# A split QKV matmul on one core: the direct columns of each pair of row blocks moved ahead of its first products

## The chip, the cores and the metric

The kernel runs on one core of a Trainium2 chip. The metric is the device time in microseconds (us) from start to end of one execution; for several executions it is the median. A profiled execution of the same program gives the trace that is read here.

## What is computed

`x` is 16 x 512 x 768 and `w_qkv` is 768 x 2304, both float32. Cut to what matters:

```python
qkv = np.matmul(x, w_qkv)                 # (16, 512, 2304)
q, k, v = qkv[..., :768], qkv[..., 768:1536], qkv[..., 1536:]
return np.stack([q, k, v], axis=0)        # (3, 16, 512, 768), float32
```

So it is one product of an 8192 x 768 matrix with a 768 x 2304 matrix, written out as three blocks of columns.

## The kernel before

**Tiles.** The 8192 rows are taken 256 at a time, as 32 "pairs" of two 128-row blocks, numbered p = 0 to 31. The 2304 columns are cut into two groups of 1024 (called q = 0 and q = 1, each two blocks of 512) and 256 columns between them, the "direct columns". For each pair and each group, `quad(p, q)`, the 2 x 2 block product (two row blocks, two halves of the inner dimension, two column blocks) is formed from seven block products instead of eight: sums of blocks of x (tile `s`, made on GpSimd) are multiplied by sums of blocks of w (`t1` to `t4`, made once). Products 1 and 2 are in bf16 and take x from the tile `xb`; products 3 to 7 are in float32r and take the sums `s`. Each product is 3 matmuls of 512 columns. The direct columns are computed plainly by `rem(p)`: 12 bf16 matmuls of 256 columns (L260), one eviction on ScalarE (L270, `orem`) and one store of 256 KB on the queue of SP (L271).

**Stages.** A prologue loads and casts w, computes pairs 0 to 2 plainly in bf16 (`block`, L396) and stores them (`store_quad`). Pairs 3 to 30 then run in a loop over p, each by `two(a, b, early)`, where a is the group q = 0 and b the group q = 1 of the same pair. Pair 31 is done by `last`. In `last`, the two halves of the direct columns follow float32r products.

**Who does what in a pair.** `do(u, n)` issues product n on TensorE (L210) and its evictions. ACT is ScalarE and DVE is VectorE.

- Product 1 opens the PSUM bank `u.x`, which ACT copies out (L224). Products 6, 7 and 4 go on accumulating into `u.x`, each after ACT has copied the state before (L231, L237, L241).
- Product 2 has its own bank `u.z`, which DVE adds to the output (L228).
- Product 5 opens the bank `u.y`. DVE adds it to the output after product 7 (L238). Product 3 then accumulates into `u.y`, so it must wait for that L238, and DVE adds it again (L244).
- `store_quad` writes a group out as two stores on SP: L251 (768 KB) and L252 (256 KB) for a, L255 (256 KB) and L256 (768 KB) for b.
- `early()` prepares x for later pairs. DVE transposes x of pair p + 1 (L130), GpSimd (POOL) rounds it to bf16 (L173, `xb`) and makes the sums (L181 to L185), and the x of pair p + 2 is loaded in four pieces of 192 KB (L126), two issued by SP and two by ACT.

**Order.** Each engine runs its instructions in the order in which the program writes them (the schedule is manual). The loads and stores of SP and ACT signal their landing on eight completion semaphores, which the layer under the kernel hands out in rotation; a transfer waits on its issuing engine until the last transfer with the same semaphore has landed. PSUM has eight banks, taken in rotation by `ps_pool`; a pair takes seven. The output tiles `o` have five buffers, `orem` two, `xin` three, `xf` two, `xb` four.

The line that makes product 3 wait, and the one that the change moves, stand in `do` and `two`:

Of the kernel before, what the change touches and what calls it, by code (L numbers as in the profile page):

```python
# [10 lines left out]
def kernel(  # L11
# [131 lines left out]
    def copy_halves(dst, src, two):  # L143

        nc.vector.tensor_copy(out=dst[0], in_=src[0])
        if two:
            nc.scalar.activation(dst[1], src[1], ident)
        else:
            nc.vector.tensor_copy(out=dst[1], in_=src[1])
# [3 lines left out]
    def cast_row(p, r, two=True):  # L153
        if r == 0:
            xc[p] = s_pool.tile([P, 2, K], bf16, name="xc", tag="s")
        halves = (slice(0, K // 2), slice(K // 2, K))
        copy_halves([xc[p][:, r, n] for n in halves], [xin[p][:, r, n] for n in halves], two)
# [41 lines left out]
    def product(u, n, ps, start):  # L199
        t1, t2, t3, t4 = ts[u.q]  # L200
        if n <= 2:
            h = (n - 1) * KH
            lhs = [xb[u.p][:, h + j, :P] for j in range(KH)]
            rhs = [b1[u.q][:, h + j, :] for j in range(KH)]
        else:
            k, t = {3: (4, b22[u.q][:]), 4: (0, t4), 5: (1, t1), 6: (2, t2), 7: (3, t3)}[n]
            lhs = [sr[u.p][:, k, j, :] for j in range(KH)]
            rhs = [t[:, j, :] for j in range(KH)]
        for j in range(KH):
            nc.tensor.matmul(  # L210
                ps[:], lhs[j], rhs[j],
                start=(start and j == 0), stop=(j == KH - 1), skip_group_check=True,
            )

    def bank():
        return ps_pool.tile([P, CB], fp32, name="ps")

    def do(u, n):
        c11, c12 = u.o[:, 0, :CB], u.o[:, 0, CB:]
        c21, c22 = u.o[:, 1, :CB], u.o[:, 1, CB:]  # L220
        if n == 1:
            u.x = bank()
            product(u, 1, u.x, True)
            nc.scalar.activation(c11, u.x[:], ident)  # L224
        elif n == 2:
            u.z = bank()
            product(u, 2, u.z, True)
            nc.vector.tensor_tensor(c11, c11, u.z[:], op=add)  # L228
        elif n == 6:
            product(u, 6, u.x, False)  # L230
            nc.scalar.activation(c12, u.x[:], ident)  # L231
        elif n == 5:
            u.y = bank()
            product(u, 5, u.y, True)
        elif n == 7:
            product(u, 7, u.x, False)
            nc.scalar.activation(c22, u.x[:], ident)  # L237
            nc.vector.tensor_tensor(c22, c22, u.y[:], op=add)  # L238
        elif n == 4:
            product(u, 4, u.x, False)  # L240
            nc.scalar.activation(c21, u.x[:], ident)  # L241
        elif n == 3:
            product(u, 3, u.y, False)
            nc.vector.tensor_tensor(c12, c12, u.y[:], op=add)  # L244

    def rows_of(s, p, lo, hi):
        return out_flat[s, p * 2 * P:(p + 1) * 2 * P, lo:hi].rearrange("(r m) n -> m r n", m=P)

    def store_quad(u):
        if u.q == 0:  # L250
            nc.sync.dma_start(rows_of(0, u.p, 0, H), u.o[:, :, :H])  # L251
            nc.sync.dma_start(rows_of(1, u.p, 0, 2 * CB - H), u.o[:, :, H:])  # L252
        else:
            part = 2 * H - Q_OFF[1]
            nc.sync.dma_start(rows_of(1, u.p, H - part, H), u.o[:, :, :part])  # L255
            nc.sync.dma_start(rows_of(2, u.p, 0, H), u.o[:, :, part:])  # L256

    def rem_row(p, r, ps):
        for j in range(KT):
            nc.tensor.matmul(  # L260
                ps, xb[p][:, j, r * P:(r + 1) * P], w_rem[j // KH][:, j % KH, :],
                start=(j == 0), stop=(j == KT - 1), skip_group_check=True,
            )

    def rem(p):
        ps = ps_pool.tile([P, 2, REM], fp32, name="ps")
        for r in range(2):
            rem_row(p, r, ps[:, r, :])
        o = or_pool.tile([P, 2, REM], fp32, name="orem")
        nc.scalar.activation(o[:], ps[:], ident)  # L270
        nc.sync.dma_start(rows_of(1, p, R_OFF - H, R_OFF - H + REM), o[:])  # L271

    def two(a, b, early):

        do(a, 1)
        do(b, 1)
        early()
        rem(a.p)
        do(a, 2)
        do(b, 2)  # L280
        do(a, 6)
        do(b, 6)
        do(a, 5)
        do(a, 7)
        do(b, 5)
        do(b, 7)
        do(a, 4)
        do(a, 3)
        store_quad(a)
        do(b, 4)  # L290
        do(b, 3)
        store_quad(b)
# [183 lines left out]
    for p in range(NS, NP):  # L476
        def early():
            if p + 1 < NP:
                transpose(p + 1)
                round_x(p + 1)  # L480
                sums_x(p + 1)
            if p + 2 < NP:
                load_x(p + 2, nc.scalar)

        if p < NP - 1:
            two(quad(p, 0), quad(p, 1), early)
        else:
            last(quad(p, 0), quad(p, 1))
# [30 lines left out]
```

## Time and profile before

| what | value |
|---|---|
| time, median of 3 runs | 362.73 us (362.62 to 362.82) |
| the profiled execution's own time | 362.66 us |
| its span, first to last instruction | 360.9 us |
| TensorE clock granted | 0.997 of full speed |
| TensorE busy | 354.3 us, 98% of the span |
| DVE, ACT, POOL busy | 224.7, 182.5, 173.5 us |
| moved by DMA | 108.08 MB, 299 GB/s over the span |

The span runs from the first to the last instruction. The time of a run is a little longer, here by 1.8 us. In the profile a line such as "L210 PE MATMUL" names the line of the kernel, the engine (PE is TensorE, PEld its weight loads) and the operation; the last letter of "SPq" or "ACTq" marks an instruction that issues a transfer. Timeline rows give the start and the length in us, and in brackets the idle time of the engine before it with what ended it. Matmul durations overlap each other, since matmuls are pipelined; the distance between starts is what a matmul costs.

### The profile page before, as it was taken

To read this page: it belongs to the slowest core of one execution; us is meant where nothing else is said; L and a number is where in the kernel's file an instruction comes from. 1 tells how busy PE (TensorE), PEld (TensorE's weight loads), DVE (VectorE), ACT (ScalarE), POOL (GpSimd) and SP (SyncE) were. 2 spreads that over 40 slices of the span, in tenths; PEclk is the share of its full clock that TensorE was granted. 3 is DMA by queue.
4 is the path that set the end of the run, shared out by engine and by line. 5 is a ranking of instruction groups with operands and counts; after the bars stand their busy time and mean duration, and the time that the engine had idled before them with its cause. 6 is when DMAs were issued, how large, how long until landed. Compare 5 with 4: busy or idle time off the path is not lost.

```text
span 360.9 us, 5252 instructions
## 1 busy us (share of the span) xinstructions
PE 354.3 (98%) x1797; PEld 250.2 (69%) x1797; DVE 224.7 (62%) x239; ACT 182.5 (51%) x304; POOL 173.5 (48%) x180
## 2 busy tenths in 40 slices
PE   7999999999999999999999999999999999999995
PEld 3544577777777777777777777777777777777763
DVE  3599736765566675566675565676556676556642
ACT  4557554545454545454545444445545454545452
POOL 0001861646664445664445665444665444666410
PEclk9999999999999999999999999999999999999998
DMA  7999969988898999999899999988989899989766
GB/s 299 404 385 369 308 224 360 316 300 293 276 330 303 291 273 296 276 319 311 283 282 287 284 303 312 293 269 297 293 285 323 295 300 271 297 263 339 274 259 235
DMA packets 80634, 108.08 MB, mean 299 GB/s; under 512 B 4833, under 2 KB 60385, under 8 KB 80609
## 3 DMA queue, kind: packets, MB, share of 16 engines
q1 hardware_dynamic: 65200, 96.35, 80.9%
q10 hardware_dynamic: 15408, 11.41, 9.6%
q8 instruction: 14, 0.23, 0.3%
q14 instruction: 12, 0.09, 0.1%
HBM read 32.24 MB, written 75.50 MB: 299 GB/s over the span
## 4 chain that ended last, share of the span: by engine, by line
PE 96%; DMA 2%; ACT 1%; ACTq 0%; SPq 0%; issue 0%; DVE 0%
PE ps L210 75%; PE ps L260 11%; PE ps L396 9%; DMA st<-in_w_qkv_dram 2%; PE ps L165 0%; ACT o L241 0%; ACTq L301 0%; SPq L141 0%; ACT orem L315 0%; DVE b L417 0%; ACTq L317 0%; ACTq L315 0%
## 5 line engine op out<-in xcount | busy, mean ns | idle before, releaser
L210 PE MATMUL ps<-t,s 128*128 128x512 f32 x696 | 173.8, 398 | 0.0
L210 PEld LDWEIGHTS ps<-t,s 128*128 128x128 f32 x696 | 130.7, 188 | 29.8
L173 POOL CAST xb<-xf 128x1536 bf16<-128x1536 f32 x29 | 43.7, 1509 | 168.2 <-DVE xf L130 166.1
L238 DVE TENSOR_TENSOR o<-o,ps 128x512 f32<-128x512 f32 x58 | 39.9, 687 | 90.9 <-ACT o L237 90.9
L130 DVE STREAM_TRANSPOSE xf<-xin 128x1536 f32<-128x1536 f32 x29 | 85.6, 2952 | 4.5 <-DMA xin<-in_x_dram 2.5
L210 PE MATMUL ps<-b,xb 128*128 128x512 bf16 x348 | 84.9, 380 | 0.0
L237 ACT ACTIVATE o<-ps 128x512 f32<-128x512 f32 x58 | 34.7, 598 | 44.3 <-PE ps L210 44.3
L210 PEld LDWEIGHTS <-xb 128*128 128x128 bf16 x348 | 31.7, 98 | 35.6 <-issue 7.3
L231 ACT ACTIVATE o<-ps 128x512 f32<-128x512 f32 x58 | 34.7, 598 | 42.3 <-PE ps L210 39.5
L244 DVE TENSOR_TENSOR o<-o,ps 128x512 f32<-128x512 f32 x58 | 39.9, 688 | 21.4 <-PE ps L210 20.2
L210 PE MATMUL ps<-b,s 128*128 128x512 f32 x174 | 48.7, 389 | 0.0
L260 PE MATMUL ps<-w_rem,xb 128*128 128x256 bf16 x384 | 47.3, 273 | 0.0
L241 ACT ACTIVATE o<-ps 128x512 f32<-128x512 f32 x58 | 34.7, 598 | 24.1 <-PE ps L210 21.3
L224 ACT ACTIVATE o<-ps 128x512 f32<-128x512 f32 x58 | 34.6, 597 | 23.8 <-DVE o L244 20.7
L260 PEld LDWEIGHTS <-xb 128*128 128x128 bf16 x384 | 37.4, 98 | 11.2 <-issue 0.5
L228 DVE TENSOR_TENSOR o<-o,ps 128x512 f32<-128x512 f32 x58 | 36.5, 671 | 4.7 <-PE ps L210 3.4
L210 PEld LDWEIGHTS ps<-b,s 128*128 128x128 f32 x174 | 32.7, 188 | 6.8
L182 POOL TENSOR_TENSOR s<-s,xf 128x384 fp32r<-128x384 f32 x29 | 30.0, 1033 | 2.3
L181 POOL TENSOR_TENSOR s<-xf 128x384 fp32r<-128x384 f32 x29 | 30.8, 1061 | 0.0
L185 POOL TENSOR_TENSOR s<-xf,s 128x384 fp32r<-128x384 f32 x29 | 29.4, 1014 | 0.0
L183 POOL TENSOR_TENSOR s<-xf 128x384 fp32r<-128x384 f32 x29 | 29.4, 1012 | 0.0
L270 ACT ACTIVATE orem<-ps 128x512 f32<-128x512 f32 x31 | 18.5, 597 | 21.2 <-PE ps L260 21.2
(36 smaller groups left out, 128.7 us busy)
## 6 DMA issues: line engine op xcount, KB each, us to landing
out_dram<-o SPq DMA_DIRECT2D x62, 768.0 KB, 5.0
out_dram<-o SPq DMA_DIRECT2D x65, 256.0 KB, 4.2
xin<-in_x_dram SPq DMA_DIRECT2D x62, 192.0 KB, 6.9
xin<-in_x_dram ACTq DMA_DIRECT2D x54, 192.0 KB, 4.4
out_dram<-orem SPq DMA_DIRECT2D x31, 256.0 KB, 5.8
st<-in_w_qkv_dram SPq DMA_DIRECT2D x6, 768.0 KB, 13.0
xin<-in_x_dram SPq DMA_DIRECT2D x3, 768.0 KB, 5.6
st<-in_w_qkv_dram SPq DMA_DIRECT2D x6, 256.0 KB, 6.0
```

Of the source, the lines that this page charges most:

```text
L130: nc.vector.transpose(t[:].rearrange("p j (g b) -> p g j b", b=G), xin.pop(p)[:].rearrange("p g (a j) -> p g j a", a=G),)
L173: nc.gpsimd.tensor_copy(out=xb[p][:], in_=xf[p][:])
L210: nc.tensor.matmul(ps[:], lhs[j], rhs[j], start=(start and j == 0), stop=(j == KH - 1), skip_group_check=True,)
L224: nc.scalar.activation(c11, u.x[:], ident)
L228: nc.vector.tensor_tensor(c11, c11, u.z[:], op=add)
L231: nc.scalar.activation(c12, u.x[:], ident)
L237: nc.scalar.activation(c22, u.x[:], ident)
L238: nc.vector.tensor_tensor(c22, c22, u.y[:], op=add)
L241: nc.scalar.activation(c21, u.x[:], ident)
L244: nc.vector.tensor_tensor(c12, c12, u.y[:], op=add)
L260: nc.tensor.matmul(ps, xb[p][:, j, r * P:(r + 1) * P], w_rem[j // KH][:, j % KH, :], start=(j == 0), stop=(j == KT - 1), skip_group_check= ...
L396: nc.tensor.matmul(ps[n][:], xb[p][:, j, r * P:(r + 1) * P], w[:, j, :], start=(j == 0), stop=(j == KT - 1), skip_group_check=True,)
```

## The change

In `two`, the call `rem(a.p)` moves from after `early()` to the very beginning:

```diff
     def two(a, b, early):
 
+        rem(a.p)
         do(a, 1)
         do(b, 1)
         early()
-        rem(a.p)
         do(a, 2)
         do(b, 2)
         do(a, 6)
```

On TensorE a pair's 12 matmuls of 256 columns now come before its first products, and its four bf16 products of 512 columns stand together, ahead of the float32r ones. On ACT the eviction L270 comes before the two L224, and these before the two load issues. On SP the store L271 comes before the two loads L126 instead of after them. DVE and POOL keep their order. The rotation of PSUM banks and of completion semaphores follows the new order, so some transfers wait for another transfer than before. The second SP load of pair p now waits for the landing of L251 of pair p - 1, which L271 waited for before. Pairs 0 to 2 and pair 31 are not touched.

## The prediction

> **What bounds the kernel now.** I began with the chain of work that ended last, on the profile's page:
>
> ```profile
> PE 96%; DMA 2%; ACT 1%; ACTq 0%; SPq 0%; issue 0%; DVE 0%
> PE ps L210 75%; PE ps L260 11%; PE ps L396 9%; DMA st<-in_w_qkv_dram 2%; PE ps L165 0%; ACT o L241 0%; ACTq L301 0%; SPq L141 0%; ACT orem L315 0%; DVE b L417 0%; ACTq L317 0%; ACTq L315 0%
> ```
>
> It is TensorE from end to end: L210 (products) and L260 (direct columns). In order of time, the same chain shows the loop's period:
>
> ```profile
> 185.94 1.31 PE ps L260 x12
> 187.25 9.43 PE ps L210 x42
> 196.68 1.31 PE ps L260 x12
> 198.00 9.43 PE ps L210 x42
> ```
>
> 1.31 + 9.43 = 10.74 us per pair with nothing in between, so in the loop TensorE never waits. Nothing can be won by taking waits away, and the change costs exactly the stalls it makes. I then looked for where a stall would come first. Per-pair windows show DVE busy 6.9 of 10.74 us, ACT 5.4, POOL 5.9, but the DMA engines 93 to 97%. The thin place is the fourth pair of rows (p = 4; its first matmul starts at 55.60, that of p = 3 at 44.84, of p = 5 at 66.34), in DVE's timeline:
>
> ```profile
> 55.79 0.69 DVE L244 TENSOR_TENSOR o<-o,ps 128x512 f32<-128x512 f32 x1 [0.67 <-PE ps L210]
> 58.43 3.02 DVE L130 STREAM_TRANSPOSE xf<-xin 128x1536 f32<-128x1536 f32 x1 [1.95 <-DMA out_dram<-orem]
> 61.39 1.23 DVE L228 TENSOR_TENSOR o<-o,ps 128x512 f32<-128x512 f32 x2
> 63.08 0.69 DVE L238 TENSOR_TENSOR o<-o,ps 128x512 f32<-128x512 f32 x1 [0.47 <-ACT o L237]
> ```
>
> The transpose of x for p = 5 waited 1.95 us for a transfer. The view names orem, but the program has it wait for the x loads, and the landing record of the second SP load is 58.21. DVE's order puts both L228 and L238 behind it. L238 ends at 63.77; the u.y bank that it reads is what `do(a, 3)` accumulates into next, and that product starts here (TensorE's timeline):
>
> ```profile
> 64.29 0.84 PE L210 MATMUL ps<-b,s 128*128 128x512 f32 x3
> ```
>
> So this transpose may be late by 0.47 (idle before L238) + 0.47 (64.29 - 63.77, less about 0.05 for the signal, an estimate from the 0.04 to 0.09 between a matmul's end and ACT's start) = **0.94 us** and no more. In steady pairs the transpose starts 0.79 us after the pair and DVE idles 2.57 before L238 (0.47 here), so the margin is 3.0.
>
> Why the load was late is in SP's timeline:
>
> ```profile
> 49.48 0.37 SPq L256 DMA_DIRECT2D out_dram<-o  x1
> 49.91 0.46 SPq L255 DMA_DIRECT2D out_dram<-o  x1
> 50.46 0.97 SPq L256 DMA_DIRECT2D out_dram<-o  x1
> 51.52 0.85 SPq L271 DMA_DIRECT2D out_dram<-orem  x1
> 52.47 2.38 SPq L126 DMA_DIRECT2D xin<-in_x_dram  x2
> 54.94 0.48 SPq L271 DMA_DIRECT2D out_dram<-orem  x1
> 55.52 0.45 SPq L251 DMA_DIRECT2D out_dram<-o  x1
> ```
>
> The first L256 (a prologue store) was ready long before; it shares a completion semaphore with the first ACT load of p = 5 (issued 46.41, landed 49.42) and waits for that landing. Everything below is queued behind it.
>
> **What the Trainium skill says.** "DMA: Bandwidth & Descriptors", section "Anatomy of one DMA — SWDGE (gpsimd) path": a semaphore wait is served on the issuing sequencer, before dispatch. The trace agrees: SP holds the whole list until 49.42. The same page, "Queues, rings and completion order": an SDMA engine takes a ring's descriptors in order, though completions need not be. Here the landings do follow SP's order (52.82, 53.53, 55.39, 56.42, 57.60, 58.21, 58.82), so a transfer put ahead delays those after it. "TensorE: Matmul & The Clock Gate", section "Back-to-back issue gap": N/2.4 + 2.5 ns, which is 216 ns for 512 columns and 109 for 256. The trace has 216 and 109 for bf16, and 227 to 232 for float32r. The same section's sustained 131 ns for 512 columns isn't seen here.
>
> **The change part by part.** Nothing is removed or added. In 28 pairs (p = 3 to 30; `last` is untouched), 12 matmuls of rem, its eviction (L270) and its store (L271) move ahead of `do(a, 1)`, `do(b, 1)` and `early()`. DVE and POOL keep their order.
>
> *TensorE.* Twelve times 109 ns move from after six products to before them: 0. The one seam that changes is float32r to bf16, now met by a 256-column product. Before, a 230 ns step and then 227 (216 + 11). In `last`, rem already follows float32r products: 230, then 120 (109 + 11). Equal extra, so 0; at most 28 x 14 ns = 0.4 us either way.
>
> *ACT.* L270 moves ahead of both L224, and both L224 and the two ACT load issues come 1.3 us later. From the steady pair that starts at 195.22, measured from its start: rem's last matmul starts at 1.21, lasts 0.27, so L270 is at 1.52 to 2.12; L224 at 2.22 to 2.81 and 2.86 to 3.46. `do(a, 6)` overwrites u.x at 3.72 and `do(b, 6)` at 4.60: margins 0.9 and 1.1. L228 starts at 3.65 as now: hidden by the transpose. Next on ACT after the issues (2.9 to about 4.2) is L231 at 4.79: free. Should an issue hold ACT past 5.4, `do(a, 7)` at 6.0 would wait.
>
> *PSUM.* Eight banks in rotation, seven taken per pair. Now rem takes the bank of y of b two pairs back, x of a that of rem, z of a that of x of b; the others are unchanged. The latest of these is read out (L241 of b) 0.1 us after the pair's start and needed by z at 2.6: 0.
>
> *SP in steady pairs.* The orem store (issue 1.2 us) goes ahead of the two SP loads, and the second load inherits the wait that orem's store had, for the 768 KB L251 of the pair before (landed 3.0 us after the pair's start). I put all x landings near 10.9, where the orem store now lands, against the transpose at 11.5 and its margin of 3. No trace shows this order; its bounds are 0 below (TensorE has no wait to win back) and the second rival above; I take 0.
>
> *SP and DVE in pairs 3 and 4*: this is the cost.
> 1. ACT load of p = 5. Before, L224 of b started at 46.39 and the issue followed at 46.41. After: rem 44.84 to 46.15, x of a and b to 47.45, L224 of b at 47.23 (last matmul) + 0.38 + 0.09 = 47.69, issue at 47.72, that is 1.31 later. Landing takes 3.0 as before (nothing competes): 50.73.
> 2. The first L256 therefore goes at 50.79, and all below it 1.31 later.
> 3. rem's store of p = 3 (256 KB) now stands before the two loads. The two orem stores of this burst landed 1.03 and 0.61 us after their forerunners; I take 0.8.
> 4. Second load lands at 58.21 + 1.31 + 0.8 = 60.3 (60.1 to 60.6); the transpose starts 0.1 to 0.2 later, at 60.5, which is 2.07 after 58.43.
> 5. Stall at `do(a, 3)`: 2.07 - 0.94 = **1.1 us** (0.8 to 1.5). The upper bound, with the slowest 256 KB store seen near here (1.29), is 1.7.
>
> What is late next: L238 of b has 0.6 to spare, POOL's cast for p = 5 ends near 65.1, before that pair starts at 67.5. Its sums end near 69.6 against 71.2. The loads for p = 6 wait for ACT loads issued 1.3 later; I find their transpose near 69, against a limit of about 71.3 in the shifted pair. So one stall, never given back, as TensorE has no idle time.
>
> **Sum.** The profiled execution took 362.66 us (span 360.9, the rest around it), 0.07 under the median of the runs, 362.73. 362.66 + 1.1 = 363.8 (363.5 to 364.4).
>
> **Rivals.** A measurement of this kernel can tell about 0.2%, 0.7 us.
>
> *Absorbed (not slower).* The load lands in time: if L256's extra wait vanished, because the ACT load lands by 49.5 after all, only orem's 0.8 would remain, below 0.94. It decides at a transpose start of 59.4. For it: the margin exists, and latencies of the same load vary from 3.0 to 7.0. Against it: an idle queue gave 3.0 before, and later issue can hardly land earlier. 362.7.
>
> *Every pair pays.* The second SP load's new wait, or an ACT issue held by a full ring, makes each pair late. At p = 4 an ACT issue took 1.31 us. Point of decision: transpose over 3.0 us late, or ACT held past 5.4. With 0.3 us over it in 27 pairs: +8, 371. Against it: the inherited landing is at 3.0, and the margins above.
>
> *Faster.* The seam vanishes or banks come free earlier. The whole seam is 0.4 us: 362.3. Against it: `last` shows it unchanged.
>
> *The change does not do what it says:* excluded, since the built program shows the moved instructions on TensorE, ACT and SP.
>
> **How the numbers follow.** One stall 0.75, absorbed 0.13, every pair 0.08, faster 0.04. Of one stall about 0.03 lies under 0.7 us; so slower 0.72 + 0.08 = 0.80, same 0.13 + 0.03 + 0.01 = 0.17, faster 0.03. The likeliest: 363.8. The range takes in absorbed and the stall's upper bound with 0.2 to spare, 362.6 to 364.6, and leaves out the last two cases, 0.12.
>
> **What the profile after would show.** Right: the first L256 at 50.8, the transpose of p = 5 near 60.5, L238 after it with no idle, a gap of about 1.1 us before `do(a, 3)` of p = 4 released by DVE L238, and then 10.74 per pair to the end. Wrong: no gap there; gaps in later pairs; a chain that leaves TensorE for ACT, SP or DMA; or pairs longer than 10.74 without a gap, which would be the seam.

## The result

The changed kernel took 364.27 us (median of 6 runs, 363.95 to 364.39) against 362.73 us (362.62 to 362.82): 1.0041 times the time before, 95% interval 1.0028 to 1.0054. That is 1.54 us slower. The forecast was 363.8 us, with a range of 362.6 to 364.6. The profiled execution took 364.25 us with a span of 362.5 us, 1.6 us longer than the span before.

The whole loss stands in one place. Two rows of the list of who waited for whom in the changed kernel (us in total, times, longest) matter. The first is the transposes' wait for x. The second is a wait of TensorE that the kernel before did not have:

```profile
DVE xf L130 <- DMA xin<-in_x_dram: 7.0, 3, 4.3
PE ps L210 <- DVE o L238: 1.3, 1, 1.3
```

One wait, once. TensorE's timeline of the changed kernel shows where; the L260 rows are the starts of pairs 4, 5 and 6, since rem now opens a pair:

```profile
55.68 1.48 PE L260 MATMUL ps<-w_rem,xb 128*128 128x256 bf16 x12
...
65.84 0.93 PE L210 MATMUL ps<-b,s 128*128 128x512 f32 x3 [1.30 <-DVE o L238]
...
67.97 1.48 PE L260 MATMUL ps<-w_rem,xb 128*128 128x256 bf16 x12
...
78.71 1.48 PE L260 MATMUL ps<-w_rem,xb 128*128 128x256 bf16 x12
```

Pair 4 lasts 67.97 - 55.68 = 12.29 us, pair 5 lasts 78.71 - 67.97 = 10.74, and every later pair 10.74, exactly as before. So the loss in the loop is 12.29 - 10.74 = 1.55 us. The 1.30 us of the row count from the end of the matmul before it. Measured from the start of its pair, the product `do(a, 3)` starts 65.84 - 55.68 = 10.16 us in, where it was 64.29 - 55.59 = 8.70 before: that is 1.46 us, and the other 0.09 go in the product itself.

The weight loads of the same product have a row too, which names POOL's cast of `xb` for p = 5:

```profile
PEld ps L210 <- POOL xb L173: 1.7, 1, 1.7
```

By the program that cast is not the cause. Product 3 of pair 4 reads the sums `s` of pair 4, not `xb` of p = 5, and POOL's last instruction for those sums (L185) ended at 50.67 + 1.01 = 51.68. The row is the same wait under another name. DVE's timeline of the same stretch:

```profile
55.87 0.69 DVE L244 TENSOR_TENSOR o<-o,ps 128x512 f32<-128x512 f32 x1 [0.67 <-PE ps L210]
60.88 3.03 DVE L130 STREAM_TRANSPOSE xf<-xin 128x1536 f32<-128x1536 f32 x1 [4.33 <-DMA xin<-in_x_dram]
63.83 1.26 DVE L228 TENSOR_TENSOR o<-o,ps 128x512 f32<-128x512 f32 x2
65.00 1.28 DVE L238 TENSOR_TENSOR o<-o,ps 128x512 f32<-128x512 f32 x2
```

The transpose of x for p = 5 waited 4.33 us where it waited 1.95, and L238 runs straight after L228, without the 0.47 us of idle time that it had. Why the load was late is in SP's timeline:

```profile
50.80 0.37 SPq L256 DMA_DIRECT2D out_dram<-o  x1
51.22 0.46 SPq L255 DMA_DIRECT2D out_dram<-o  x1
51.77 0.97 SPq L256 DMA_DIRECT2D out_dram<-o  x1
52.84 2.16 SPq L271 DMA_DIRECT2D out_dram<-orem  x2
55.09 1.72 SPq L126 DMA_DIRECT2D xin<-in_x_dram  x2
56.91 0.50 SPq L251 DMA_DIRECT2D out_dram<-o  x1
```

The first L256 is issued at 50.80 (49.48 before), and there are now two orem stores (L271 x2) ahead of the two loads. The second load landed at 60.66 (58.21 before).

What the first L256 waits for is in SP's list of waits, here before, then after the change. ACT's timeline of the changed kernel has the load that it waits for, the first of p = 5 on ACT, issued at 46.41 before:

```profile
SPq L256 <- DMA xin<-in_x_dram: 6.7, 1, 6.7
```

```profile
SPq L256 <- DMA xin<-in_x_dram: 8.0, 1, 8.0
```

```profile
47.79 0.89 ACTq L126 DMA_DIRECT2D xin<-in_x_dram  x2
```

In all eight traces of this document, this L256 is issued 63 or 64 ns after the landing of that load, wherever the load stands.

### The profile page after: what moved, and what is told of

It is laid out like the page before. It is cut to its first block, busy times and chain, and to the rows that moved or that the text cites. A ratio compares the mean times of both kernels' runs of the same rounds, so it can differ in the third digit from the quotient of the medians.

```text
span 362.5 us, 5190 instructions
## 1 busy us (share of the span) xinstructions
PE 353.7 (98%) x1764; PEld 250.8 (69%) x1797; DVE 224.2 (62%) x239; ACT 182.2 (50%) x304; POOL 173.5 (48%) x180
## 3 DMA queue, kind: packets, MB, share of 16 engines
q10 hardware_dynamic: 15408, 11.41, 10.9%
## 4 chain that ended last, share of the span: by engine, by line
PE 94%; issue 1%; DMA 1%; DVE 1%; ACT 1%; ACTq 0%; SPq 0%; DVEq 0%
PE ps L210 72%; PE ps L260 11%; PE ps L396 9%; PE ps L371 1%; DMA xin<-in_x_dram 1%; PE ps L165 1%; DVE o L228 0%; ACT o L241 0%; ACTq L301 0%; SPq L126 0%; ACT orem L315 0%; DVE o L244 0%; DVE o L238 0%; ACTq L317 0%; DVE xb L145 0%
## 5 line engine op out<-in xcount | busy, mean ns | idle before, releaser
L238 DVE TENSOR_TENSOR o<-o,ps 128x512 f32<-128x512 f32 x58 | 39.8, 687 | 89.3 <-ACT o L237 89.3
L210 PE MATMUL ps<-b,xb 128*128 128x512 bf16 x319 | 78.3, 379 | 1.6
L260 PE MATMUL ps<-w_rem,xb 128*128 128x256 bf16 x384 | 47.5, 273 | 0.0
L260 PEld LDWEIGHTS <-xb 128*128 128x128 bf16 x384 | 35.2, 98 | 11.7 <-issue 7.6
L270 ACT ACTIVATE orem<-ps 128x512 f32<-128x512 f32 x31 | 18.5, 597 | 42.4 <-PE ps L260 40.6
L228 DVE TENSOR_TENSOR o<-o,ps 128x512 f32<-128x512 f32 x58 | 36.3, 663 | 5.0 <-ACT o L224 4.1
L224 ACT ACTIVATE o<-ps 128x512 f32<-128x512 f32 x58 | 34.5, 597 | 3.6 <-DVE o L244 0.8
L185 POOL TENSOR_TENSOR s<-xf,s 128x384 fp32r<-128x384 f32 x29 | 29.5, 1016 | 0.0
```

Source lines behind the costliest of these rows:

```text
L210: nc.tensor.matmul(ps[:], lhs[j], rhs[j], start=(start and j == 0), stop=(j == KH - 1), skip_group_check=True,)
L260: nc.tensor.matmul(ps, xb[p][:, j, r * P:(r + 1) * P], w_rem[j // KH][:, j % KH, :], start=(j == 0), stop=(j == KT - 1), skip_group_check= ...
```

## The experiments

All use the names of the kernel; the edits are against the kernel before, except the last two, which are against the changed kernel. Lines that are added shift the line numbers in a few of them. Two questions were open: is the loss one event or a little in every pair, and which of the two delays in pair 3 makes it.

**Only pair 3, or all but pair 3.**

```diff
     def two(a, b, early):
+        if a.p > 3:          # the other kernel: a.p == 3
+            rem(a.p)
         do(a, 1)
         do(b, 1)
         early()
-        rem(a.p)
+        if a.p == 3:         # the other kernel: a.p > 3
+            rem(a.p)
```

Without pair 3 in the new order (e1):

> The new order in pairs 4 to 30, the old one in pair 3 alone. Theory (one stall in pair 4, caused by pair 3's order on ACT and SP): the transpose of p = 5 starts near 58.4 as before, no wait ahead of do(a, 3) of pair 4, 10.74 us per pair, 362.7 us. Rival (every pair pays, 1.5 us / 28 = 0.055 us each, through the seam or the banks): 27/28 of the loss stays, 364.2 us.

Measured: 362.62 us against 362.66, ratio 0.9999 (0.9991 to 1.0007). Every pair of the loop takes 10.74 us in its trace, and DVE's timeline is that of the kernel before:

```profile
58.40 3.02 DVE L130 STREAM_TRANSPOSE xf<-xin 128x1536 f32<-128x1536 f32 x1 [1.95 <-DMA xin<-in_x_dram]
61.34 1.25 DVE L228 TENSOR_TENSOR o<-o,ps 128x512 f32<-128x512 f32 x2
63.06 0.69 DVE L238 TENSOR_TENSOR o<-o,ps 128x512 f32<-128x512 f32 x1 [0.46 <-ACT o L237]
```

Pair 3 alone in the new order (e2):

> The new order in pair 3 alone, the old one in pairs 4 to 30. Theory: the whole loss, transpose of p = 5 near 60.9, a wait of about 1.3 us ahead of do(a, 3) of pair 4, 364.2 to 364.3 us. Rival (every pair pays): 1/28 of the loss, 362.8 us.

Measured: 364.41 us, ratio 1.0048 (1.0036 to 1.0061). DVE's and TensorE's rows:

```profile
61.01 3.07 DVE L130 STREAM_TRANSPOSE xf<-xin 128x1536 f32<-128x1536 f32 x1 [4.55 <-DMA xin<-in_x_dram]
```

```profile
65.99 0.93 PE L210 MATMUL ps<-b,s 128*128 128x512 f32 x3 [1.56 <-DVE o L238]
```

So 27 pairs of the new order cost nothing, and one costs everything. The rival that every pair pays has fallen: neither the seam on TensorE, nor the banks, nor the moved wait of the second SP load costs any time that can be seen in the steady pairs. The change in pair 3 alone took 0.14 us longer than the whole change. In its trace the ACT loads of pair 4, left in their old place, are issued at 57.15 in place of 58.50, and the first SP load of p = 5 lands at 60.32 in place of 59.84, the second at 60.78 in place of 60.66. That the earlier ACT loads hold it up fits this but was not tried by itself.

**The two delays apart.** In pair 3 alone, the first kernel keeps rem's matmuls and eviction ahead but leaves its store behind the loads (e3). The second keeps ACT's and TensorE's old order but puts the store ahead of the two SP loads (e4).

```diff
# e3: rem's store apart from rem
-        rem(a.p)
+        if a.p == 3:  o = rem(a.p, False)   # stands ahead of do(a, 1); no store
...
+        if a.p == 3:  rem_store(a.p, o)     # after early(); other pairs: rem(a.p) here
# e4: in early(), for p == 3 (and two() then leaves rem out)
+                load_x(p + 2, nc.scalar, (1,))   # the two ACT loads
+                rem(p)
+                load_x(p + 2, nc.scalar, (0,))   # the two SP loads
```

> In pair 3 alone rem's matmuls and eviction come first, but its store is issued after the two SP loads, as before; other pairs keep the old order. So only the later ACT loads act (first L256 at 50.8 in place of 49.5), not the store ahead of the loads. Theory (the two delays add, and only what exceeds the 0.94 us margin costs): second SP load lands near 59.6, transpose near 59.8, stall 1.3 - 0.94 + 0.25 (signal and restart, as in the changed kernel) = 0.6, 363.2 to 363.4 us. Rival (the store ahead is all of the cost): 362.7 us.

Measured: 363.25 us against 362.66, ratio 1.0015 (1.0009 to 1.0022). The second load landed at 59.67. DVE, then TensorE:

```profile
59.89 3.06 DVE L130 STREAM_TRANSPOSE xf<-xin 128x1536 f32<-128x1536 f32 x1 [3.26 <-DMA out_dram<-orem]
```

```profile
64.86 0.93 PE L210 MATMUL ps<-b,s 128*128 128x512 f32 x3 [0.26 <-DVE o L238]
```

The DVE row names orem, as the view of the kernel before does. The orem store behind the loads landed at 60.24, after this transpose had started, so the wait is for the load.

> In pair 3 alone the ACT loads, the matmuls and the eviction of rem stand as before, but rem's store is issued ahead of the two SP loads; other pairs keep the old order. Theory: first L256 at 49.5, second SP load lands 0.9 to 1.1 later than before, at 59.1 to 59.3, transpose near 59.4, all inside the margin or just over it: stall 0 to 0.3, 362.7 to 363.0 us. Rival (the later ACT loads are not needed for the loss): 364.2 us.

Measured: 362.94 us, ratio 1.0007 (0.9999 to 1.0016), so from the time alone it is not clear of no change. The trace is clearer: the second load landed at 59.27, and `do(a, 3)` starts at 64.48, against 64.29 before, though the gap is too short to be marked. Line numbers are one higher here. SP, DVE and TensorE:

```profile
51.56 2.14 SPq L272 DMA_DIRECT2D out_dram<-orem  x2
53.80 1.75 SPq L127 DMA_DIRECT2D xin<-in_x_dram  x2
```

```profile
59.49 3.08 DVE L131 STREAM_TRANSPOSE xf<-xin 128x1536 f32<-128x1536 f32 x1 [3.05 <-DMA xin<-in_x_dram]
```

```profile
64.48 0.93 PE L211 MATMUL ps<-b,s 128*128 128x512 f32 x3
```

Neither delay is the loss by itself. From the start of pair 4 in each trace, the second load lands 1.31 us later with the later ACT loads alone, 1.10 with the store ahead alone, and 2.37 with both, close to their sum of 2.41. Beyond a fixed margin, each further microsecond costs about a microsecond:

| kernel | transpose of p = 5, after pair 4's start | length of pair 4 | lost in pair 4 | that start, less 3.63 |
|---|---|---|---|---|
| before | 2.84 | 10.74 | 0 | none |
| store ahead alone (e4) | 3.93 | 11.07 | 0.33 | 0.30 |
| later ACT loads alone (e3) | 4.14 | 11.26 | 0.52 | 0.51 |
| the change | 5.20 | 12.29 | 1.55 | 1.57 |
| the change in pair 3 alone (e2) | 5.44 | 12.55 | 1.81 | 1.81 |

The figure 3.63 is chosen to fit the last four rows. Less 2.84 it makes a margin of about 0.8 us.

**The change with its loads earlier.** If the late load of p = 5 is the whole cause, issuing it sooner must bring back all the time with rem still at the head of every pair.

```diff
# e5: all pairs; e6: the same for p == 3 alone
         def early():
             ...
-            if p + 2 < NP:
-                load_x(p + 2, nc.scalar)
...
+        if p + 2 < NP:
+            load_x(p + 2, nc.scalar)
         if p < NP - 1:
             two(quad(p, 0), quad(p, 1), early)
```

> The change as it is in all pairs, but the x loads of pair p + 2 are issued at the top of each pair, ahead of rem, instead of in early(). Theory: the first ACT load of p = 5 is issued near 45.1 and lands near 48.1, the first L256 goes then, all below it 1.4 us earlier than in the kernel before and with rem's store again behind the two loads; the transpose of p = 5 is no later than 58.4, no wait ahead of do(a, 3), 10.74 us per pair, 362.7 us. Rival (rem at the head is itself the cost, by the order on TensorE or the banks): 364.2 us.

Measured: 362.64 us against 362.64, ratio 1.0 (0.9991 to 1.0008). SP's first row, then DVE's, of the kernel with all loads first:

```profile
48.12 0.37 SPq L256 DMA_DIRECT2D out_dram<-o  x1
```

```profile
57.14 2.98 DVE L130 STREAM_TRANSPOSE xf<-xin 128x1536 f32<-128x1536 f32 x1 [0.68 <-DMA out_dram<-orem]
60.04 1.24 DVE L228 TENSOR_TENSOR o<-o,ps 128x512 f32<-128x512 f32 x2
63.06 0.69 DVE L238 TENSOR_TENSOR o<-o,ps 128x512 f32<-128x512 f32 x1 [1.77 <-ACT o L237]
```

The first L256 again follows the landing of the first ACT load of p = 5, now at 48.05. (The transpose's row names orem once more; that store landed at 57.60, after the transpose had started.)

> The change as it is in all pairs; only the x load of p = 5 in pair 3 is moved to the top of that pair. Theory: as with all loads first, 362.7 us and no wait in pair 4, which puts the whole loss on this one load. Rival (later pairs need their loads early too): a wait in a later pair, 363.0 us or more.

Measured: 362.66 us, ratio 1.0 (0.9992 to 1.0008); the transpose of p = 5 starts at 57.31 and L238 has 1.73 us of idle time ahead of it. So four pieces of one load, issued earlier, pay for the whole change. The weak place even becomes wider than it was before, 1.77 in place of 0.47, and yet the time is only that of the kernel before: with no TensorE wait in the loop there was nothing more to win. No version came out faster than the kernel before.

## Why the prediction was right, point by point

- *TensorE bounds the loop, so the change costs its stalls alone.* Shown: pairs of 10.74 us in every kernel, apart from pair 4.
- *TensorE's seam, PSUM, ACT: 0.* Shown together by e1, where 27 pairs have all of them and the time does not move. They were not tried one by one. (The float32r steps in the trace before run from 224 to 236 ns, most of them 226 or 227, a little wider than the 227 to 232 that I read; no term rests on it.)
- *SP in steady pairs: 0.* This was taken between two bounds, with no trace of the new order. The loads are in fact later there too: from pair 5 on, the second one landed 10.5 to 11.3 us after the start of the pair that issues it (10.1 to 10.7 before; I had put it near 10.9). That is still ahead of the next transpose, at 10.74 + 0.80 = 11.54. The transpose starts 0.80 us after the pair's start in nearly all later pairs of both kernels. Pair 5 is the exception, with 1.39 in the changed kernel and 1.17 before, far inside the limit of 3.63.
- *Steps 1 and 2, the ACT load 1.31 later and L256 behind it.* The ACT load was issued at 47.79 (predicted 47.72, and the pair itself began 0.08 later here) and landed 2.94 us on; L256 went at 50.80 (predicted 50.79). By itself this delay measured 1.31 (e3).
- *Step 3, the store ahead of the loads: sized too low.* I took 0.8 us from the landing steps of the two orem stores. By itself it measured 1.10 (e4). In that trace the orem store of p = 3 landed 1.03 after its forerunner (the transfer before it), which itself landed 0.21 sooner after the start of pair 4 than before. The two loads behind it then took steps of 1.36 and 0.71, where before they took 1.19 and 0.61; I had counted no such growth. SP also issued the second load 1.21 us later (54.96 against 53.75), so the runs do not tell how much of the delay is SP's issuing and how much the transfers.
- *Step 4.* The transpose started at 60.88, not 60.5. Most of the difference is step 3.
- *Step 5, the margin: sized too high.* I had 0.94; the table gives about 0.8. L238 of a ends at 65.00 + 0.69 = 65.69 and the matmul starts at 65.84, a signal of 0.15 where I took 0.05. And TensorE lost 0.09 on starting again: from `do(a, 3)` to the next pair it took 67.97 - 65.84 = 2.13 us, where before it took 66.33 - 64.29 = 2.04. DVE won back 0.06: L238 now starts 65.00 - 60.88 = 4.12 us after the transpose, and before it was 63.08 - 58.43 = 4.65, of which 0.47 idle, so 4.18. Put together, 0.94 - 0.10 - 0.09 + 0.06 = 0.81.
- *Sum.* 2.37 - 0.8 is about 1.6, near the 1.55 measured, against the forecast's 2.07 - 0.94 = 1.1. Both terms were off to the same side, by 0.3 and 0.14, so they did not make up for each other. The 1.55 us lost in pair 4 are just above the 0.8 to 1.5 given for the stall, and below its bound of 1.7. The mechanism and its place were right.
- *Absorbed* fell with the transpose at 60.88: it asked for one before 59.4, and for an ACT load landed by 49.5, where it was 50.73. *Every pair pays* fell with e1. *Faster* has no trace in any run.

## What to carry to other kernels

Where one engine is the chain from end to end and never waits, as here, moving independent work on it has nothing to win; look at what the move does to the queues of the other engines, transfers first. Look for the weak place also in the stretch where the loop is entered, not in its steady state alone: here one pair had 0.8 us to spare and the others, by the same limit, 2 us or more. A wait handed on through a shared completion semaphore made a store depend on a load that it has nothing to do with, and everything behind that store on the same queue with it. What cured it here was to issue the loads that the next stage needs ahead of work whose results are merely leaving.

## What was not expected of the hardware

A 256 KB store put ahead of two 192 KB loads held up the second by 1.10 us, a little more than the 1.03 us by which that store itself landed after its forerunner (e4). In all four kernels that lost time (the change, e2, e3, e4), the TensorE product that had to wait started 0.15 us after the end of the DVE instruction that released it, and its three matmuls then took 0.09 to 0.10 us longer than in the kernel before. A store that waited on SP for another transfer's semaphore was issued 63 or 64 ns after that transfer's landing, in all eight traces.
